# Batched 64x64 matrix products: the transpose of A moves from TensorE to 32x32 blocks on VectorE, with A loaded in tiles of 64 matrices

## The chip, the cores and the metric

The kernel runs on one core of one Trainium2 chip. The metric is the device time of one execution in microseconds (us); lower is better. Engines in the profile: PE is TensorE (PEld its weight loads), DVE is VectorE, ACT is ScalarE, POOL is GpSimd, SP is the engine that only issues transfers. SP, ACT and POOL each issue DMAs into a queue of their own: q1 is SP's, q10 is ACT's, q0 is POOL's. [...]

## The reference

```python
def setup_inputs():
    return {
        "a": np.random.randn(1024, 64, 64).astype(np.float32),
        "b": np.random.randn(1024, 64, 64).astype(np.float32),
    }

def reference(a, b):
    return np.matmul(a, b).astype(np.float32)
```

There are 1024 products of 64x64 matrices. Each of a, b and the output is 16.78 MB.

## The kernel before, in words

The batch is worked in 16 tiles of 64 matrices (index t). One TensorE multiply handles four matrices at once: the contraction index k is kept as 32 pairs of bf16 numbers (a pair is moved about as one fp32 word), four matrices times 32 pairs fill the 128 partitions, and the stationary operand is a block diagonal `at_bd` that holds the transposed a of those four matrices, with zeros elsewhere. The moving operand is b in bf16, `b_bf`. For each group of four there are two row halves (j) and two members of the pair (u), so 64 multiplies (L189) for each tile.

*a* comes in super-tiles of 128 matrices (index s, two tiles each). A super-tile has four parts h of 512 KB. `load_a` (L69) loads three parts with a cast to bf16 on POOL's queue (L73) and one part raw, in fp32, on SP's queue (L77). The first super-tile comes raw in all four parts, two on SP and two on ACT (L90). Every run that is read is 4 KB. `regroup` (L99) puts the parts together in one bf16 tile `a_bf`: for s = 0 by two copies each on VectorE and ScalarE (L105), else by two VectorE copies (L108, L111). `transpose` then uses TensorE with an identity (L120), eight 128x128 fp32 transposes for each half j, into PSUM, and ScalarE copies them out to `at_sb` (L123). `spread` (L133) copies `at_sb` into the block diagonal, four VectorE copies of 32 partitions for each tile. Two block diagonals are used in turn.

*b* comes one tile at a time, 1 MB, even tiles on SP and odd tiles on ACT (L96), with three buffers. `cast` turns it into bf16 on VectorE (L144), for the first tile on ScalarE, for the last tile in quarters on both (L149, L151).

*The output.* `multiply` writes two PSUM tiles for each t. Each is evacuated by four copies of 64x512 into `o_sb` (L177), on ScalarE but for two in each odd tile, which are VectorE's. `store` sends 1 MB for each tile from POOL's queue (L166), the last two tiles from SP and ACT in pieces. There are eight `o_sb` buffers.

The order of the instructions on every engine is the order of the program text: the schedule is written out by hand under `manual_schedule`, and each engine works its own list in order, waiting where its data isn't there. In the loop over t the next tile's spread and cast come first, then the loads further ahead, then `multiply(t)`, then regrouping and transposes for later super-tiles, then the store of tile t-1.

Of the kernel before, what the change touches and what calls it, by code (L numbers as in the profile page):

```python
# [7 lines left out]

fp32 = mybir.dt.float32
# [4 lines left out]
def kernel(  # L14
# [8 lines left out]

    nc = tc.nc
    B, M, K = a.shape  # L30
    _, _, N = b.shape
    assert (M, K, N) == (64, 64, 64) and B % 128 == 0

    n_t, n_s = B // 64, B // 128
    A_AHEAD = 3
    B_AHEAD = 3
    N_BD = 2
    HOLD = 2

    a_v = a.rearrange("(s g h) (mp v) k -> s h g mp (v k)", h=4, g=32, v=16)  # L40
    b_v = b.rearrange("(t g h) (kp u) n -> t (h kp) g (u n)", h=4, g=16, u=2)
    o_v = out.rearrange("(t gh x) (mo w) n -> t (x mo) gh (w n)", gh=8, x=8, w=4)

    consts = ctx.enter_context(tc.tile_pool(name="consts", bufs=1))
    a_pool = ctx.enter_context(tc.tile_pool(name="a_pool", bufs=A_AHEAD))
    b_pool = ctx.enter_context(tc.tile_pool(name="b_pool", bufs=B_AHEAD))
    work = ctx.enter_context(tc.tile_pool(name="work", bufs=2))
    o_pool = ctx.enter_context(tc.tile_pool(name="o_pool", bufs=8))
    t_psum = ctx.enter_context(
        tc.tile_pool(name="t_psum", bufs=4, space=bass.MemoryType.PSUM)  # L50
    )
    o_psum = ctx.enter_context(
        tc.tile_pool(name="o_psum", bufs=2, space=bass.MemoryType.PSUM)
    )

    bd_tiles = [
        consts.tile([128, 2, 16, 2, 4, 16], fp32, name=f"at_bd{i}") for i in range(N_BD)
    ]
    identity = consts.tile([128, 128], fp32)
    warm = consts.tile([128, 2], fp32)  # L60
    a_tiles, b_tiles, abf_tiles, at_tiles, bbf_tiles = {}, {}, {}, {}, {}
    held = {}

    def store_queue(t, lo):
        if t < n_t - 2:
            return nc.gpsimd
        return nc.scalar if t == n_t - 1 and lo % 4 == 0 else nc.sync

    def load_a(s):  # L69

        a_sb = a_pool.tile([128, 3, 16, 64], bf16, name="a_sb")
        for h in range(3):
            nc.gpsimd.dma_start(  # L73
                out=a_sb[:, h, :, :].rearrange("p v k -> p (v k)"), in_=a_v[s, h], single_packet=True
            )
        a_raw = a_pool.tile([128, 16, 64], fp32, name="a_raw")
        nc.sync.dma_start(out=a_raw[:].rearrange("p v k -> p (v k)"), in_=a_v[s, 3])  # L77
        a_tiles[s] = a_sb, a_raw

    def load_first_a():  # L80

        raw = [
            o_pool.tile([128, 8, 2, 2, 64], fp32, name="o_sb")[:].rearrange(
                "p gh j wl n -> p (gh j wl n)"
            )
            for _ in range(2)
        ]
        parts = [raw[h % 2][:, 1024 * (h // 2) : 1024 * (h // 2) + 1024] for h in range(4)]
        for h in range(4):
            (nc.scalar if h % 2 else nc.sync).dma_start(out=parts[h], in_=a_v[0, h])  # L90
        a_tiles[0] = parts

    def load_b(t):
        b_sb = b_pool.tile([128, 16, 128], fp32, name="b_sb")
# [1 line left out]
        queue.dma_start(out=b_sb[:], in_=b_v[t])  # L96
        b_tiles[t] = b_sb

    def regroup(s):  # L99
        a_sb = a_tiles.pop(s)  # L100
        a_bf = work.tile([128, 16, 4, 64], bf16, name="a_bf")
        if s == 0:
            for h in range(4):
                copy = nc.scalar.copy if h % 2 else nc.vector.tensor_copy
                copy(a_bf[:, :, h, :], a_sb[h].rearrange("p (v k) -> p v k", v=16))  # L105
        else:
            cast_sb, raw = a_sb
            nc.vector.tensor_copy(  # L108
                a_bf[:, :, 0:3, :], cast_sb[:].rearrange("p h v k -> p v h k")
            )  # L110
            nc.vector.tensor_copy(a_bf[:, :, 3, :], raw[:])  # L111
        abf_tiles[s] = a_bf
        at_tiles[s] = work.tile([128, 2, 32, 2, 4, 4], fp32, name="at_sb")

    def transpose(s, j):
        a_cols = abf_tiles[s][:].rearrange("p v h k -> p v (h k)").bitcast(fp32)
        for wl in range(2):
            at_ps = t_psum.tile([128, 4, 128], fp32, name="at_ps")
            for vo in range(4):
                nc.tensor.transpose(  # L120
                    at_ps[:, vo, :], a_cols[:, 4 * vo + 2 * j + wl, :], identity[:]
                )
            nc.scalar.copy(  # L123
                at_tiles[s][:, j, :, wl, :, :],
                at_ps[:].rearrange("p vo (g mp) -> p g mp vo", mp=4),
            )

    def spread(t):
        half = slice(16 * (t % 2), 16 * (t % 2) + 16)
        bd = bd_tiles[t % N_BD]  # L130
        for h in range(4):
            rows = slice(32 * h, 32 * h + 32)
            nc.vector.tensor_copy(  # L133
                bd[rows, :, :, :, h, :].rearrange("p j g wl mo -> p j (g wl) mo"),
                at_tiles[t // 2][rows, :, half, :, :, :].rearrange(
                    "p j g wl mp vo -> p j (g wl) (mp vo)"
                ),
            )

    def cast(t):  # L140
# [15 lines left out]
            piece()  # L156

    def multiply(t):
        at_bd = bd_tiles[t % N_BD][:].rearrange("p j g wl h mo -> p j g (wl h mo)")
        at_bd = at_bd.bitcast(bf16).rearrange("p j g (c u) -> p j g c u", u=2)  # L160
        b_bf = bbf_tiles.pop(t)
        last = t == n_t - 1
# [6 lines left out]
            )  # L169

        def evacuate(o_ps, gh, n, copies):

            for par in range(2):
                for wl in range(2):
                    src = o_ps[64 * wl : 64 * wl + 64, :, par, :, :]
                    dst = o_sb[64 * par : 64 * par + 64, gh : gh + n, :, wl, :]
                    copies[2 * par + wl](dst, src)  # L177

        for half in range(2):
            if not last:  # L180
                o_ps = o_psum.tile([128, 4, 2, 2, 64], fp32, name="o_ps")
            for g8 in range(8):
                if last and g8 % 4 == 0:
                    o_ps = t_psum.tile([128, 2, 2, 2, 64], fp32, name="at_ps")
                g = 8 * half + g8
                gl = (g8 % 4 if last else g8) // 2
                for j in range(2):
                    for u in range(2):
                        nc.tensor.matmul(  # L189
                            o_ps[:, gl, g % 2, j, :],  # L190
                            at_bd[:, j, g, :, u],
                            b_bf[:, g, 64 * u : 64 * u + 64],
                            start=(u == 0),
                            stop=(u == 1),
                        )
                if last and g8 % 4 == 3:
                    copy = nc.scalar.copy if g8 == 3 else nc.vector.tensor_copy
                    evacuate(o_ps, g // 4 * 2, 2, [copy] * 4)
            if not last:
                copies = [nc.scalar.copy] * 4  # L200
                if half and t % 2:
                    copies[2:] = [nc.vector.tensor_copy] * 2
                evacuate(o_ps, 4 * half, 4, copies)
        if last:
            held[t] = [lambda q=q: put(2 * q, 2) for q in range(4)]
        else:
# [1 line left out]
            held[t] = [lambda q=q: put(q, 8 if whole else 4) for q in ([0] if whole else [0, 4])]  # L208

    with tc.manual_schedule():  # L210
        load_first_a()

        nc.vector.memset(warm[:, 0:1], 0.0)
        nc.scalar.copy(warm[:, 1:2], warm[:, 0:1])  # L214
        load_b(0)
        load_b(1)
        nc.vector.memset(bd_tiles[0][:], 0.0)  # L217
        make_identity(nc, identity)
        nc.gpsimd.memset(bd_tiles[1][:, 0], 0.0)
        load_a(1)  # L220
        load_b(2)
        nc.gpsimd.memset(bd_tiles[1][:, 1], 0.0)
        load_a(2)
        regroup(0)
        transpose(0, 0)
        transpose(0, 1)
        spread(0)
        cast(0)
        for t in range(n_t):
            s, half = t // 2, t % 2  # L230
            if t + 1 < n_t:
                spread(t + 1)
                cast(t + 1)
            if t + B_AHEAD < n_t:
                load_b(t + B_AHEAD)
            if half == 0 and 0 < s < n_s - 1 - A_AHEAD:
                load_a(s + 1 + A_AHEAD)
            if half == 0 and 0 < s < n_s - 1:
                transpose(s + 1, 1)
            multiply(t)  # L240
            if t == 0:
                regroup(1)
                load_a(A_AHEAD)
                load_a(A_AHEAD + 1)
                transpose(1, 0)
                transpose(1, 1)
            elif t == 1:
                regroup(2)
            elif half == 0 and s + 2 < n_s:
                regroup(s + 2)  # L250
            if half == 1 and s + 2 < n_s:
                transpose(s + 2, 0)
            if t >= HOLD - 1:
                store(t - HOLD + 1)
        for t in range(n_t - HOLD + 1, n_t):
            store(t)
# [30 lines left out]
```

## Time and profile before

| | |
|---|---|
| time, median of 3 runs | 134.95 us (134.95 to 135.0) |
| span of the profiled execution, first to last instruction | 133.4 us |
| time of the profiled execution itself | not given apart from its span |
| busy: PE, DVE, ACT, POOL | 64.4, 94.6, 87.9, 33.0 us |
| moved in HBM | 33.55 MB read, 16.78 MB written |
| mean granted TensorE clock | 0.785 of full |

A group row of the page reads: line, engine, operation, output <- input, shapes, count, then busy us and mean ns of one, then the idle time of the engine just before these instructions and what ended most of it. In the strip of 40 slices each digit is a busy share in tenths.

### The profile page before, as it was taken

To read this page: it belongs to the slowest core of one execution; us is meant where nothing else is said; L and a number is where in the kernel's file an instruction comes from. 1 tells how busy PE (TensorE), PEld (TensorE's weight loads), DVE (VectorE), ACT (ScalarE), POOL (GpSimd) and SP (SyncE) were. 2 spreads that over 40 slices of the span, in tenths; PEclk is the share of its full clock that TensorE was granted. 3 is DMA by queue.
4 is the path that set the end of the run, shared out by engine and by line. 5 is a ranking of instruction groups with operands and counts; after the bars stand their busy time and mean duration, and the time that the engine had idled before them with its cause. 6 is when DMAs were issued, how large, how long until landed. Compare 5 with 4: busy or idle time off the path is not lost.

```text
span 133.4 us, 2837 instructions
## 1 busy us (share of the span) xinstructions
PE 64.4 (48%) x1152; PEld 61.1 (46%) x1152; DVE 94.6 (71%) x120; ACT 87.9 (66%) x161; POOL 33.0 (25%) x43
## 2 busy tenths in 40 slices
PE   0006406960089384289518970956197363970000
PEld 0006306950089274189418950945196363960000
DVE  5930399109998809995999699959999995987000
ACT  3225424999036998969595969696968969099600
POOL 8991000420090070341233021203020410300000
PEclk9999975797557999856985699599959955599555
DMA  3999999999999999999999999999999999999990
GB/s 77 371 329 311 307 311 281 284 306 325 327 312 401 316 320 333 399 384 397 311 281 375 406 389 351 304 316 390 394 396 387 396 392 391 402 405 398 382 319 18
DMA packets 19021, 45.01 MB, mean 337 GB/s; under 512 B 1088, under 2 KB 3136, under 8 KB 19008
## 3 DMA queue, kind: packets, MB, share of 16 engines
q0 software_dynamic: 6832, 20.19, 50.1%
q1 hardware_dynamic: 7120, 14.68, 30.4%
q10 hardware_dynamic: 5056, 9.96, 19.7%
q8 instruction: 9, 0.15, 0.4%
q14 instruction: 4, 0.03, 0.1%
HBM read 33.55 MB, written 16.78 MB: 377 GB/s over the span
## 4 chain that ended last, share of the span: by engine, by line
DMA 53%; DVE 15%; ACT 13%; PE 6%; issue 5%; SPq 2%; DVEq 0%; ACTq 0%
DMA b_sb<-in_b_dram 53%; ACT o_sb L177 9%; DVE at_bd L133 6%; PE o_ps L189 4%; DVE b_bf L144 4%; DVE o_sb L177 3%; PE at_ps L120 2%; ACT at_sb L123 2%; ACT b_bf L144 1%; SPq L90 1%; DVE a_bf L108 1%; SPq L96 1%; ACT b_bf L151 1%; DVE a_bf L111 0%; SPq L77 0%
## 5 line engine op out<-in xcount | busy, mean ns | idle before, releaser
L177 ACT COPY o_sb<-o_ps 64x512 f32<-64x512 f32 x106 | 61.5, 580 | 10.3 <-PE o_ps L189 9.0
L189 PEld LDWEIGHTS <-at_bd 128*128 128x128 bf16 x1024 | 42.3, 113 | 39.5 <-DVE b_bf L144 25.7
L189 PE MATMUL o_ps<-b_bf,at_bd 128*128 128x64 bf16 x960 | 42.6, 216 | 35.4 <-DVE b_bf L144 23.4
L133 DVE COPY at_bd<-at_sb 32x1024 f32<-32x1024 f32 x64 | 46.9, 733 | 14.1 <-ACT at_sb L123 11.8
L120 PE MATMUL at_ps<-identity,a_bf 128*128 128x128 f32 x128 | 21.2, 335 | 19.4 <-ACT a_bf L105 11.2
L166 POOL DMA_DIRECT2D out_dram<-o_sb x14 | 15.4, 1097 | 56.9 <-ACT at_sb L123 23.4
L120 PEld LDWEIGHTS at_ps<-identity,a_bf 128*128 128x128 f32 x128 | 19.3, 180 | 19.5 <-issue 19.5
L123 ACT COPY at_sb<-at_ps 128x512 f32<-128x512 f32 x32 | 17.5, 590 | 11.0 <-PE at_ps L120 7.8
L144 DVE CAST b_bf<-b_sb 128x2048 bf16<-128x2048 f32 x14 | 17.8, 1271 | 9.6 <-DMA b_sb<-in_b_dram 9.4
L73 POOL DMA_DIRECT2D a_sb<-in_a_dram x21 | 13.6, 662 | 26.4 <-DVE a_bf L108 19.4
L177 DVE COPY o_sb<-o_ps 64x512 f32<-64x512 f32 x14 | 9.7, 690 | 0.3
L108 DVE COPY a_bf<-a_sb 128x3072 bf16<-128x3072 bf16 x7 | 6.7, 950 | 0.0
L105 ACT CAST a_bf<-o_sb 128x1024 bf16<-128x1024 f32 x2 | 2.1, 1044 | 5.2 <-DMA o_sb<-in_a_dram 5.2
L111 DVE CAST a_bf<-a_raw 128x1024 bf16<-128x1024 f32 x7 | 4.8, 683 | 0.0
L144 ACT CAST b_bf<-b_sb 128x2048 bf16<-128x2048 f32 x1 | 1.9, 1900 | 3.9 <-DMA b_sb<-in_b_dram 3.9
L105 DVE CAST a_bf<-o_sb 128x1024 bf16<-128x1024 f32 x2 | 2.8, 1382 | 1.9 <-DMA o_sb<-in_a_dram 1.9
L217 DVE MEMSET at_bd<- 128x4096 f32 x1 | 3.5, 3472 | 0.8 <-issue 0.8
L177 DVE COPY o_sb<-at_ps 64x256 f32<-64x256 f32 x8 | 3.4, 422 | 0.5 <-PE at_ps L189 0.4
L151 ACT CAST b_bf<-b_sb 128x512 bf16<-128x512 f32 x2 | 1.1, 615 | 3.6 <-DMA b_sb<-in_b_dram 3.6
L177 ACT COPY o_sb<-at_ps 64x256 f32<-64x256 f32 x8 | 2.9, 366 | 0.1
L214 ACT ACT_TABLE_LOAD x1 | 1.3, 1283 | 2.3 <-issue 2.3
L189 PE MATMUL at_ps<-b_bf,at_bd 128*128 128x64 bf16 x64 | 2.0, 193 | 1.0 <-DVE at_bd L133 1.0
(12 smaller groups left out, 6.1 us busy)
## 6 DMA issues: line engine op xcount, KB each, us to landing
out_dram<-o_sb POOLq DMA_DIRECT2D x14, 1024.0 KB, 21.6
a_sb<-in_a_dram POOLq DMA_DIRECT2D x21, 256.0 KB, 16.4
a_raw<-in_a_dram SPq DMA_DIRECT2D x7, 512.0 KB, 18.7
o_sb<-in_a_dram SPq DMA_DIRECT2D x2, 512.0 KB, 5.9
o_sb<-in_a_dram ACTq DMA_DIRECT2D x2, 512.0 KB, 7.1
out_dram<-o_sb SPq DMA_DIRECT2D x2, 512.0 KB, 7.5
out_dram<-o_sb SPq DMA_DIRECT2D x2, 256.0 KB, 7.8
out_dram<-o_sb ACTq DMA_DIRECT2D x2, 256.0 KB, 5.5
```

The costliest lines, as they stand in the source:

```text
L73: nc.gpsimd.dma_start(out=a_sb[:, h, :, :].rearrange("p v k -> p (v k)"), in_=a_v[s, h], single_packet=True)
L105: copy(a_bf[:, :, h, :], a_sb[h].rearrange("p (v k) -> p v k", v=16))
L108: nc.vector.tensor_copy(a_bf[:, :, 0:3, :], cast_sb[:].rearrange("p h v k -> p v h k"))
L111: nc.vector.tensor_copy(a_bf[:, :, 3, :], raw[:])
L120: nc.tensor.transpose(at_ps[:, vo, :], a_cols[:, 4 * vo + 2 * j + wl, :], identity[:])
L123: nc.scalar.copy(at_tiles[s][:, j, :, wl, :, :], at_ps[:].rearrange("p vo (g mp) -> p g mp vo", mp=4),)
L133: nc.vector.tensor_copy(bd[rows, :, :, :, h, :].rearrange("p j g wl mo -> p j (g wl) mo"), at_tiles[t // 2][rows, :, half, :, :, :].rearrange(
L144: (nc.vector.tensor_copy if t else nc.scalar.copy)(b_bf[:], b_sb[:])
L166: store_queue(t, lo).dma_start(out=o_v[t, :, lo : lo + n, :], in_=o_sb[:, lo : lo + n].rearrange("p gh j wl n -> p (gh j wl n)"),)
L177: copies[2 * par + wl](dst, src)
L189: nc.tensor.matmul(o_ps[:, gl, g % 2, j, :], at_bd[:, j, g, :, u], b_bf[:, g, 64 * u : 64 * u + 64], start=(u == 0), stop=(u == 1),)
L217: nc.vector.memset(bd_tiles[0][:], 0.0)
```

## The change

The super-tile of 128 matrices is given up: a comes tile by tile, 64 matrices in two parts h of 512 KB. The partition order of a part is now (q mp g) and no longer (g mp): the 32 partitions of one quadrant hold four row blocks mp of eight matrices, so that a 32x32 block transpose within a quadrant brings the pairs of k onto the partitions. VectorE does this transpose, one instruction for each part over 128 partitions and 512 fp32 words, and writes it so that the four `spread` copies read one contiguous stretch. TensorE's transposes, the identity, the PSUM tiles for them, ScalarE's copies out of PSUM and `regroup` are gone.

Ten of the 32 parts come raw (both of tile 0, the second of each odd tile) in a pool of three buffers, and are cast by ScalarE (one by VectorE); the other 22 are cast on POOL's queue. Loads of a run six tiles ahead; before, three super-tiles. All evacuations but those of the last tile are on ScalarE. PSUM has three output tiles in place of two, and two smaller ones for the last tile. In the start, POOL's casting loads come ahead of its memsets.

```diff
-    A_AHEAD = 3
+    A_AHEAD = 6
+    RAW = [(0, 0), (0, 1)] + [(t, 1) for t in range(1, n_t, 2)]
-    a_v = a.rearrange("(s g h) (mp v) k -> s h g mp (v k)", h=4, g=32, v=16)
+    a_v = a.rearrange("(t h g q) (mp v) k -> t h (q mp) g (v k)", h=2, g=8, q=4, mp=4)
...
+    def load_a(t):
+        a_tiles[t] = a_pool.tile([128, 2, 16, 64], bf16, name="a_sb")
+        for h in range(2):
+            if (t, h) in RAW:
+                raw = raw_pool.tile([128, 16, 64], fp32, name="a_raw")
+                raw_tiles[t, h] = raw
+                queue = nc.scalar if t == 0 and h else nc.sync
+                queue.dma_start(out=raw[:].rearrange("p v k -> p (v k)"), in_=a_v[t, h])
+            else:
+                nc.gpsimd.dma_start(
+                    out=a_tiles[t][:, h].rearrange("p v k -> p (v k)"),
+                    in_=a_v[t, h],
+                    single_packet=True,
+                )
...
+    def transpose(t):
+        a_sb = a_tiles.pop(t)
+        at_tiles[t] = work.tile([128, 2, 8, 4, 4, 4], fp32, name="at_sb")
+        for h in range(2):
+            if (t, h) in RAW:
+                copy = nc.vector.tensor_copy if t == 0 and not h else nc.scalar.copy
+                copy(a_sb[:, h], raw_tiles.pop((t, h))[:])
+            pairs = a_sb[:, h].rearrange("p v k -> p (v k)").bitcast(fp32)
+            nc.vector.transpose(
+                at_tiles[t][:, h].rearrange("p g w mp vo -> p w vo mp g"),
+                pairs.rearrange("p (vo w kp) -> p w vo kp", vo=4, w=4),
+            )
+
+    def spread(t):
+        bd = bd_tiles[t % N_BD]
+        at_sb = at_tiles.pop(t)
+        for q in range(4):
+            rows = slice(32 * q, 32 * q + 32)
             nc.vector.tensor_copy(
+                bd[rows, :, :, q, :, :].rearrange("p g w mp vo -> p (g w) (mp vo)"),
+                at_sb[rows].rearrange("p h g w mp vo -> p (h g w) (mp vo)"),
             )
...
-                copies = [nc.scalar.copy] * 4
-                if half and t % 2:
-                    copies[2:] = [nc.vector.tensor_copy] * 2
-                evacuate(o_ps, 4 * half, 4, copies)
+                evacuate(o_ps, 4 * half, 4, [nc.scalar.copy] * 4)
...
     with tc.manual_schedule():
+        load_a(0)
         nc.vector.memset(warm[:, 0:1], 0.0)
         nc.scalar.copy(warm[:, 1:2], warm[:, 0:1])
         load_b(0)
+        load_a(1)
         load_b(1)
         nc.vector.memset(bd_tiles[0][:], 0.0)
         load_b(2)
         load_a(2)
+        nc.gpsimd.memset(bd_tiles[1][:, 0:8], 0.0)
+        load_a(3)
+        nc.gpsimd.memset(bd_tiles[1][:, 8:16], 0.0)
+        load_a(4)
+        load_a(5)
+        transpose(0)
         spread(0)
         cast(0)
+        transpose(1)
         for t in range(n_t):
             if t + 1 < n_t:
                 spread(t + 1)
                 cast(t + 1)
+            if t + 2 < n_t:
+                transpose(t + 2)
             if t + B_AHEAD < n_t:
                 load_b(t + B_AHEAD)
+            if t + A_AHEAD < n_t:
+                load_a(t + A_AHEAD)
             multiply(t)
             if t >= HOLD - 1:
                 store(t - HOLD + 1)
```

More of the change, by code (lines that the diff above doesn't have):

```diff
@@ L5 @@
 from concourse import bass_utils, mybir
-from concourse.masks import make_identity
 from concourse._compat import with_exitstack
@@ L31 @@
     _, _, N = b.shape
-    assert (M, K, N) == (64, 64, 64) and B % 128 == 0
-    n_t, n_s = B // 64, B // 128
-    A_AHEAD = 3
+    assert (M, K, N) == (64, 64, 64) and B % 64 == 0
+    n_t = B // 64
+    A_AHEAD = 6
     B_AHEAD = 3
@@ L38 @@
     HOLD = 2
-    a_v = a.rearrange("(s g h) (mp v) k -> s h g mp (v k)", h=4, g=32, v=16)
-    b_v = b.rearrange("(t g h) (kp u) n -> t (h kp) g (u n)", h=4, g=16, u=2)
+    RAW = [(0, 0), (0, 1)] + [(t, 1) for t in range(1, n_t, 2)]
+    a_v = a.rearrange("(t h g q) (mp v) k -> t h (q mp) g (v k)", h=2, g=8, q=4, mp=4)
+    b_v = b.rearrange("(t g q) (kp u) n -> t (q kp) g (u n)", q=4, g=16, u=2)
     o_v = out.rearrange("(t gh x) (mo w) n -> t (x mo) gh (w n)", gh=8, x=8, w=4)
@@ L45 @@
     a_pool = ctx.enter_context(tc.tile_pool(name="a_pool", bufs=A_AHEAD))
+    raw_pool = ctx.enter_context(tc.tile_pool(name="raw_pool", bufs=3))
     b_pool = ctx.enter_context(tc.tile_pool(name="b_pool", bufs=B_AHEAD))
@@ L48 @@
     o_pool = ctx.enter_context(tc.tile_pool(name="o_pool", bufs=8))
-    t_psum = ctx.enter_context(
-        tc.tile_pool(name="t_psum", bufs=4, space=bass.MemoryType.PSUM)
-    )
-    o_psum = ctx.enter_context(
-        tc.tile_pool(name="o_psum", bufs=2, space=bass.MemoryType.PSUM)
+    o_psum = ctx.enter_context(
+        tc.tile_pool(name="o_psum", bufs=3, space=bass.MemoryType.PSUM)
+    )
+    q_psum = ctx.enter_context(
+        tc.tile_pool(name="q_psum", bufs=2, space=bass.MemoryType.PSUM)
     )
     bd_tiles = [
-        consts.tile([128, 2, 16, 2, 4, 16], fp32, name=f"at_bd{i}") for i in range(N_BD)
+        consts.tile([128, 16, 4, 4, 4, 4], fp32, name=f"at_bd{i}") for i in range(N_BD)
     ]
-    identity = consts.tile([128, 128], fp32)
     warm = consts.tile([128, 2], fp32)
-    a_tiles, b_tiles, abf_tiles, at_tiles, bbf_tiles = {}, {}, {}, {}, {}
-    held = {}
+    a_tiles, raw_tiles, at_tiles = {}, {}, {}
+    b_tiles, bbf_tiles, held = {}, {}, {}
     def store_queue(t, lo):
@@ L67, in store_queue @@
         return nc.scalar if t == n_t - 1 and lo % 4 == 0 else nc.sync
[L69 to L91, printed above, removed]
+    def load_a(t):
[12 more added lines that the diff above has]
+                )
     def load_b(t):
@@ L97, in load_b @@
         b_tiles[t] = b_sb
[L99 to L125, printed above, removed]
+    def transpose(t):
[9 more added lines that the diff above has]
+                pairs.rearrange("p (vo w kp) -> p w vo kp", vo=4, w=4),
@@ L126, in transpose @@
             )
     def spread(t):
-        half = slice(16 * (t % 2), 16 * (t % 2) + 16)
         bd = bd_tiles[t % N_BD]
-        for h in range(4):
-            rows = slice(32 * h, 32 * h + 32)
+        at_sb = at_tiles.pop(t)
+        for q in range(4):
+            rows = slice(32 * q, 32 * q + 32)
             nc.vector.tensor_copy(
[L134 to L137, printed above, removed]
+                bd[rows, :, :, q, :, :].rearrange("p g w mp vo -> p (g w) (mp vo)"),
+                at_sb[rows].rearrange("p h g w mp vo -> p (h g w) (mp vo)"),
@@ L158, in multiply @@
     def multiply(t):
-        at_bd = bd_tiles[t % N_BD][:].rearrange("p j g wl h mo -> p j g (wl h mo)")
+        at_bd = bd_tiles[t % N_BD][:].rearrange("p g (j wl) q mp vo -> p j g (wl q mp vo)", j=2)
         at_bd = at_bd.bitcast(bf16).rearrange("p j g (c u) -> p j g c u", u=2)
@@ L183, in multiply @@
                 if last and g8 % 4 == 0:
-                    o_ps = t_psum.tile([128, 2, 2, 2, 64], fp32, name="at_ps")
+                    o_ps = q_psum.tile([128, 2, 2, 2, 64], fp32, name="q_ps")
                 g = 8 * half + g8
@@ L210 @@
     with tc.manual_schedule():
-        load_first_a()
+        load_a(0)
         nc.vector.memset(warm[:, 0:1], 0.0)
@@ L215 @@
         load_b(0)
+        load_a(1)
         load_b(1)
         nc.vector.memset(bd_tiles[0][:], 0.0)
-        make_identity(nc, identity)
-        nc.gpsimd.memset(bd_tiles[1][:, 0], 0.0)
-        load_a(1)
         load_b(2)
-        nc.gpsimd.memset(bd_tiles[1][:, 1], 0.0)
         load_a(2)
-        regroup(0)
-        transpose(0, 0)
-        transpose(0, 1)
+        nc.gpsimd.memset(bd_tiles[1][:, 0:8], 0.0)
[4 more added lines that the diff above has]
+        transpose(0)
         spread(0)
         cast(0)
+        transpose(1)
         for t in range(n_t):
-            s, half = t // 2, t % 2
             if t + 1 < n_t:
@@ L233 @@
                 cast(t + 1)
+            if t + 2 < n_t:
+                transpose(t + 2)
             if t + B_AHEAD < n_t:
                 load_b(t + B_AHEAD)
[L236 to L239, printed above, removed]
+            if t + A_AHEAD < n_t:
+                load_a(t + A_AHEAD)
             multiply(t)
[L241 to L252, printed above, removed]
             if t >= HOLD - 1:
```

## The prediction

> **What bounds the kernel now.** I read the page's strip of 40 slices first, then the queue table, then the windows of the DMA engines, then the chain of waits.
>
> ```profile
> DMA  3999999999999999999999999999999999999990
> HBM read 33.55 MB, written 16.78 MB: 377 GB/s over the span
> ```
>
> The DMA engines are busy from the first slices to the last but one: 50.33 MB (33.55 + 16.78) in a span of 133.4 us. The windows (columns: stretch, length, busy us of PE, PEld, DVE, ACT and POOL, PE clock, DMA share, GB/s) show whether that is a steady rate:
>
> ```profile
> 2.00:5.00 3.00, 0.00 (x0) 0.00 (x0) 3.00 (x1) 1.47 (x3) 3.00 (x5) 1.00 0.90 259
> 10.00:20.00 10.00, 3.60 (x16) 3.38 (x17) 4.36 (x7) 4.10 (x6) 0.53 (x1) 0.90 1.08 310
> 90.00:100.00 10.00, 6.04 (x132) 5.83 (x133) 9.71 (x13) 7.78 (x15) 2.30 (x2) 0.83 1.03 393
> 100.00:110.00 10.00, 5.94 (x120) 5.49 (x119) 9.68 (x13) 8.26 (x17) 1.90 (x2) 0.84 1.03 391
> 117.00:124.00 7.00, 2.22 (x68) 1.97 (x65) 5.21 (x12) 6.82 (x14) 0.00 (x0) 0.99 1.02 400
> 129.00:133.40 4.40, 0.00 (x0) 0.00 (x0) 0.00 (x0) 0.00 (x0) 0.00 (x0) 0.50 0.19 68
> ```
>
> The GB/s count what is written. A casting load reads twice what it writes: the software queue wrote 0.93 MB of casts in 10 to 20 us, so 3.10 + 0.93 = 4.03 MB were read or stored, 403 GB/s. So every full stretch shown stands at 391 to 403, whatever the mix. With 398, 50.33 MB take 126.5 us. The other 6.9 us lie at the ends: before 5 us 0.78 MB moved (worth 2.0 us, so 3.0 lost), after 129 us 0.30 MB (4.4 less 0.75, so 3.65 lost). Start, transfers, end: 3.0 + 126.5 + 3.65 = 133.2 of 133.4.
>
> How the queues share, in 15 to 20 us (columns: packets, MB, share of 16 engines' time):
>
> ```profile
> q0 software_dynamic: 257, 0.46, 48.7%
> q1 hardware_dynamic: 257, 0.65, 36.2%
> q10 hardware_dynamic: 235, 0.45, 23.6%
> ```
>
> Busy queues get equal packets. In 117 to 124 us q0 alone has 97% and the rate stays at 400, so one queue that is never empty is enough.
>
> The end is a chain behind the last load: b of tile 15 is awaited by L151 until 116.88, and the span ends 16.5 us later. All DMA ends about 130 too, so both run out together. Hence the rule that I use: span = the later of (start + 126.5 + end) and (last load used + 16.5).
>
> **Engines, part by part.** The rows that price the change:
>
> ```profile
> L177 ACT COPY o_sb<-o_ps 64x512 f32<-64x512 f32 x106 | 61.5, 580 | 10.3 <-PE o_ps L189 9.0
> L133 DVE COPY at_bd<-at_sb 32x1024 f32<-32x1024 f32 x64 | 46.9, 733 | 14.1 <-ACT at_sb L123 11.8
> L120 PE MATMUL at_ps<-identity,a_bf 128*128 128x128 f32 x128 | 21.2, 335 | 19.4 <-ACT a_bf L105 11.2
> L123 ACT COPY at_sb<-at_ps 128x512 f32<-128x512 f32 x32 | 17.5, 590 | 11.0 <-PE at_ps L120 7.8
> L144 DVE CAST b_bf<-b_sb 128x2048 bf16<-128x2048 f32 x14 | 17.8, 1271 | 9.6 <-DMA b_sb<-in_b_dram 9.4
> L177 DVE COPY o_sb<-o_ps 64x512 f32<-64x512 f32 x14 | 9.7, 690 | 0.3
> L111 DVE CAST a_bf<-a_raw 128x1024 bf16<-128x1024 f32 x7 | 4.8, 683 | 0.0
> ```
>
> *TensorE* loses 128 transposes, 64.4 - 21.2 = 43.2 us. It bounds nothing; worth nothing.
>
> *ScalarE* loses L123 (17.5) and two casts at L105 (2.1), and gains 14 evacuations (8.1) and nine raw casts at L105's 1.04 (9.4): 87.9 becomes 85.8. Per tile 8 x 0.580 + half of 1.04 = 5.2 us. The raw cast now stands ahead of a tile's evacuations, so a late raw load would hold these; it is issued four tiles early, and such loads landed in 18.7 us at the median.
>
> *VectorE* loses L108 (6.7), L111 (4.8), L105 (2.8) and 14 evacuations (9.7). It gains one raw cast (0.7) and 32 block transposes of 128x512 fp32, which no row shows. Below, they are bounded by half of the 128x1024 cast at L111, 0.34 us; above, by the slowest copy of up to 1024 elements, one L105 cast of 2.07 us. The row of as many elements read once is the evacuation of 64x512 at 0.69 us, and I take it: 32 x 0.69 = 22.1. DVE: 94.6 - 24.0 + 22.8 = 93.4 us. Per tile: 4 x 0.733 + 1.27 + 2 x 0.69 = 5.6 us; with 0.34, 4.9; with 2.07, 8.3.
>
> [...]
>
> *The spread* keeps its 64 copies at 0.73 us, in runs of 16 elements on both sides as before.
>
> **Transfers.** Bytes read and written in HBM are the same; one 512 KB part of a turns from raw to cast (22 casts, 10 raw). From the shares in 15 to 20 us a cast packet (4 KB read) costs 0.487 x 16 x 5 / 257 = 152 ns; a 4 KB store packet in 90 to 100 us (61.1% for 611 packets) costs 0.611 x 160 / 611 = 160 ns. Nothing to gain or lose. Runs stay 4 KB; their order in HBM changes. No row prices that. For all 16.78 MB of a (42.2 us) I bound it by the spread of the rates shown, 391 to 403, 3% or 1.3 us either way, and take zero, since no mix shown left that band.
>
> *Start.* POOL's first cast is issued at 3.00 us, behind the identity and a memset, and q0 moved nothing before 5 us. Now it is POOL's first work, about 0.7 us, so its packets can fill the 0.19 MB missing in 3 to 5 us: 0.5 us gained (bounds 0 and the whole hole of 2 to 5 us, 1.05).
>
> *Do the engines still feed the queues?* SP moved 2.1 MB until b of tile 0 landed at 19.26, about 121 GB/s; now half of that a goes ahead of it, 1.57 MB, 13 us, so tile 0 multiplies near 17 instead of 21.24. Loads ahead are six tiles of a and three of b, 9.4 MB or 24 us: enough. Then engines need 5.6 us a tile and DMA 50.33 / 16 / 0.398 = 7.9, so DMA sets the pace. In one software queue the casts for tile u+2 stand behind stores up to u-6. So at tile 13, a whole (16.8), b of 15 tiles (15.7) and 8 stores (8.4) must have moved: 40.9 MB, 3.0 + 102.8 = 105.8 us (before, this multiply began at 107.8). One DVE tile later, 111.4, b of tile 15 is cast, against 116.88 now; plus 16.5 is 127.9, under the DMA's end. So the end is pure DMA, with the last stores issued earlier into a full queue. Of the 3.65 us at the end, the ragged part is at most the 2 us before the wait after the last packet; I take 0.4.
>
> DMA_DIRECT2D for casts and stores stay on POOL (21 + 14 become 22 + 14, 0.66 us each for the casts), raw loads on SP (now eight more than the first tile's, before seven); a raw load waiting for its three buffers holds SP's next b, but those buffers are freed two tiles after landing. [...] Measured: in 90 to 100 us DVE was busy 9.71 of 10 and q0 moved 2.33 MB at a DMA share of 1.03. [...]
>
> **Sum.** 133.4 - 0.5 (start) - 0.4 (end) = 132.5. The runs' median, 134.95, lies 1.55 above the span (the page gives no time of its own for the profiled execution, so I take that one at the median): 134.05, said as 134.1.
>
> **Rivals.**
> 1. *Nothing moves.* The holes at both ends are latencies, not late issues: 134.95. For it: q10 and q1 were both loaded from 0.75 us, yet nothing moved before 2 us. What a measurement can tell is 0.2%, 0.27 us. Chance 0.13.
> 2. *Slower by slow transposes.* The strided writes double the row's 0.69 or worse. DVE waits become the pace when tile 15's cast comes after 117: (117 - 19) / 14 = 7.0 us a tile, that is (7.0 - 4.2) / 2 = 1.4 us a transpose. Each 0.1 us beyond costs 28 x 0.1 = 2.8 us: 1.5 gives 138, 2.07 gives 154. Against: one read and one write per element in every row near. Chance 0.13.
> 3. *Slower by late casts.* DVE's transpose waits in line ahead of the next spread and cast of b, PE and ACT behind it. Before, the casts were up to eight tiles ahead; now six, and their slowest landing was 29 us. If they take that, plus 8 us behind a store's wait, five tiles last 37 us, 7.4 each: tile 15 at 17 + 14 x 7.4 = 120.6, span 137.1, time 138.6; half-way, 136.5. Against: while q0 is late it gets more of the engines, as in 117 to 124. Chance 0.17.
> 4. *The order of a in HBM counts.* 1.3 us: 135.4 when worse (0.07), 132.8 when better, within the forecast's cases.
>
> **Numbers.** My forecast (faster, 132 to 134.7) gets 0.50. Faster 0.50, same 0.13, slower 0.13 + 0.17 + 0.07 = 0.37. Range: low is 134.95 less 1.05 and 2.0, 131.9, said as 132.0; the high end takes in rival 3 and the transposes up to 1.5 us: 138.6. The forecast's own range is 132.0 to 134.7.
>
> **What would show it.** DMA share above 1.0 from 5 to 129 us; q0 with packets before 4 us; tile 0's multiply near 17; transposes at 0.6 to 0.8 us; DVE near 93; the last cast of b before 117. Wrong if the transposes exceed 1.4 us, if DMA falls under 1.0 in mid-span, or if full stretches leave 391 to 403 GB/s.

## The result, and the profile after

The changed kernel takes 140.91 us (median of 4 runs, 140.02 to 142.28) against 134.97. The run at 142.28 was in a slower state of the chip, so the differences below use the median of the other three, 140.55. The change makes the kernel slower by 5.6 us, a ratio of 1.041 (95% interval 1.036 to 1.045). Forecast were 134.1 us and a range up to 138.6. The profiled execution has a span of 138.6 us and a time of its own of 140.55; the span before was 133.4.

Two lines of the page, first the DMA strip, then what was moved:

```profile
DMA  3999999999999999999999999999999999999993
HBM read 33.55 MB, written 16.78 MB: 363 GB/s over the span
```

The strip looks as it did: busy from end to end. The bytes are the same too. They only moved at 363 GB/s of the span where it was 377. The windows of the changed kernel (columns as in the prediction) say where:

```profile
5.00:10.00 5.00, 0.00 (x0) 0.00 (x0) 4.18 (x4) 1.04 (x1) 3.79 (x5) 1.00 1.07 255
10.00:20.00 10.00, 0.00 (x0) 0.10 (x1) 3.82 (x6) 0.74 (x1) 1.24 (x2) 1.00 1.09 292
100.00:110.00 10.00, 4.29 (x78) 3.97 (x75) 8.96 (x12) 7.71 (x15) 0.89 (x1) 0.50 1.06 337
117.00:124.00 7.00, 3.93 (x91) 3.69 (x88) 6.38 (x12) 5.17 (x9) 0.89 (x1) 0.74 1.03 407
129.00:138.60 9.60, 0.00 (x0) 0.00 (x0) 0.00 (x0) 0.00 (x0) 0.00 (x0) 0.50 0.81 276
```

The DMA share is above 1.0 in every full stretch, as forecast. But the rate has left the band. In 10 to 20 us POOL's queue wrote 0.91 MB, all of it casts, so 2.92 + 0.91 = 3.83 MB were read, 383 GB/s against 403 before. In 5 to 10 us it is 1.27 + 0.45 = 1.72 MB, 344 GB/s, against 1.81 + 0.25 = 2.06 MB and 412. Once all of a has been loaded, in 117 to 124 us, the rate is 407, as good as the 400 before. The engines of DMA are as busy as they were and get less done while a is being loaded. They do so in some stretches more than in others. In 40 to 50 us the packet records of the trace have 0.54 MB of casts before the change and 0.42 MB after it, so with these lines, first before and then after, the rates are 400 and 342:

```profile
40.00:50.00 10.00, 7.20 (x149) 6.76 (x147) 5.55 (x7) 8.61 (x15) 2.89 (x5) 0.90 1.06 346
```

```profile
40.00:50.00 10.00, 4.97 (x88) 4.55 (x86) 8.06 (x11) 9.75 (x18) 3.41 (x5) 1.00 1.06 300
```

The queue view shows it packet by packet. ACT's queue carries nothing but b in 30 to 40 us, in packets of 2 KB, and b's loads are the same in both kernels. First the kernel before, then the changed one (columns: packets, MB, share of 16 engines' time):

```profile
DMA packets 1305, 3.21 MB, mean 321 GB/s; under 512 B 128, under 2 KB 128, under 8 KB 1305
...
q10 hardware_dynamic: 300, 0.58, 15.2%
```

```profile
DMA packets 1200, 3.29 MB, mean 329 GB/s; under 512 B 79, under 2 KB 79, under 8 KB 1199
...
q10 hardware_dynamic: 342, 0.67, 24.1%
```

The share times 160 us (16 engines for 10 us), divided by the packets, is the mean time of one. A packet of b takes 0.152 x 160 / 300 = 0.081 us before and 0.241 x 160 / 342 = 0.113 us after. GB/s alone can't be compared here, since the mix of casts and stores differs; the time of one packet of the same load can. Over the whole run the packet records of the trace give the same: raw packets of 4 KB on SP's queue 198 ns (176 before), tile 0's raw part on ACT's queue 281 (167 for the two there before), b on ACT's queue 98 (86), casts 172 and 172. (The shares give a little less, as in the prediction's 152 ns for a cast: they also count the packets of 4 bytes, 16 for each load or store, at 9 to 16 ns each.)

The engines did what the groups were to show, with one exception:

```profile
L146 ACT COPY o_sb<-o_ps 64x512 f32<-64x512 f32 x120 | 69.6, 580 | 10.6 <-PE o_ps L158 9.0
L105 DVE COPY at_bd<-at_sb 32x1024 f32<-32x1024 f32 x64 | 44.5, 695 | 2.3
L95 DVE STREAM_TRANSPOSE at_sb<-a_sb 128x512 f32<-128x512 f32 x32 | 32.6, 1079 | 10.9 <-ACT a_sb L93 10.8
```

The evacuations cost 580 ns each as before. The block transposes cost 1.08 us, not 0.69, so VectorE is busy for 102.9 us and not 93.4.

### The profile page after: what moved, and what is told of

It is laid out like the page before. It is cut to its first block, busy times and chain, and to the rows that moved or that the text cites. A ratio compares the mean times of both kernels' runs of the same rounds, so it can differ in the third digit from the quotient of the medians.

```text
span 138.6 us, 2542 instructions
## 1 busy us (share of the span) xinstructions
PE 54.3 (39%) x1024; PEld 51.7 (37%) x1024; DVE 102.9 (74%) x123; ACT 86.6 (62%) x150; POOL 31.1 (22%) x42
## 4 chain that ended last, share of the span: by engine, by line
DMA 74%; DVE 9%; ACT 8%; issue 1%; PE 1%; DVEq 0%; SPq 0%; ACTq 0%
DMA b_sb<-in_b_dram 50%; DMA a_raw<-in_a_dram 24%; ACT o_sb L146 6%; DVE b_bf L114 4%; DVE at_sb L95 2%; DVE at_bd L105 2%; ACT a_sb L93 2%; DVE o_sb L146 1%; PE q_ps L158 1%; ACT b_bf L121 0%; DVEq L235 0%; ACT b_sb L84 0%; SPq L84 0%; DVEq L105 0%; ACTq L121 0%
## 5 line engine op out<-in xcount | busy, mean ns | idle before, releaser
L158 PEld LDWEIGHTS <-at_bd 128*128 128x128 bf16 x1024 | 51.7, 126 | 75.4 <-DVE b_bf L114 42.9
L158 PE MATMUL o_ps<-b_bf,at_bd 128*128 128x64 bf16 x960 | 51.2, 235 | 68.6 <-DVE b_bf L114 44.3
L146 ACT COPY o_sb<-o_ps 64x512 f32<-64x512 f32 x120 | 69.6, 580 | 10.6 <-PE o_ps L158 9.0
L105 DVE COPY at_bd<-at_sb 32x1024 f32<-32x1024 f32 x64 | 44.5, 695 | 2.3
L95 DVE STREAM_TRANSPOSE at_sb<-a_sb 128x512 f32<-128x512 f32 x32 | 32.6, 1079 | 10.9 <-ACT a_sb L93 10.8
L93 ACT CAST a_sb<-a_raw 128x1024 bf16<-128x1024 f32 x9 | 9.4, 1046 | 13.7 <-DMA a_raw<-in_a_dram 13.5
L146 DVE COPY o_sb<-q_ps 64x256 f32<-64x256 f32 x8 | 3.4, 422 | 3.5 <-PE q_ps L158 3.4
L158 PE MATMUL q_ps<-b_bf,at_bd 128*128 128x64 bf16 x64 | 3.1, 216 | 4.3 <-DVE o_sb L146 1.9
L146 ACT COPY o_sb<-q_ps 64x256 f32<-64x256 f32 x8 | 2.9, 367 | 0.1
L121 ACT CAST b_bf<-b_sb 128x512 bf16<-128x512 f32 x2 | 1.1, 617 | 2.0 <-DMA b_sb<-in_b_dram 2.0
L188 POOL MEMSET at_bd<- 128x2048 f32 x1 | 1.9, 1863 | 0.0
L186 POOL MEMSET at_bd<- 128x2048 f32 x1 | 1.8, 1848 | 0.0
```

What stands on the lines that cost most here:

```text
L93: copy(a_sb[:, h], raw_tiles.pop((t, h))[:])
L95: nc.vector.transpose(at_tiles[t][:, h].rearrange("p g w mp vo -> p w vo mp g"), pairs.rearrange("p (vo w kp) -> p w vo kp", vo=4, w=4),)
L105: nc.vector.tensor_copy(bd[rows, :, :, q, :, :].rearrange("p g w mp vo -> p (g w) (mp vo)"), at_sb[rows].rearrange("p h g w mp vo -> p (h ...
L158: nc.tensor.matmul(o_ps[:, gl, g % 2, j, :], at_bd[:, j, g, :, u], b_bf[:, g, 64 * u : 64 * u + 64], start=(u == 0), stop=(u == 1),)
L186: nc.gpsimd.memset(bd_tiles[1][:, 0:8], 0.0)
L188: nc.gpsimd.memset(bd_tiles[1][:, 8:16], 0.0)
```

## The experiments

Two theories stood at first. *Transfer theory*: the order in which a is read slows the DMA engines; nothing else matters. *Engine theory*: the longer transposes and ScalarE's waits for raw parts pace the loads. In the diffs below `a_v` is the view of a that the loads read; the first dimension that steps over partitions is called outer, the second inner. Except with runs of 2 KB, a kernel that reads a in another order multiplies permuted rows and doesn't give the reference's output: it measures the loads and is no replacement.

**All parts contiguous.** Only the order of a's 4 KB pieces is altered.

```diff
-    a_v = a.rearrange("(t h g q) (mp v) k -> t h (q mp) g (v k)", h=2, g=8, q=4, mp=4)
+    a_v = a.rearrange("(t h g q) (mp v) k -> t h (g q mp) (v k)", h=2, g=8, q=4, mp=4)
```

> The changed kernel, with only the order in which the parts of a are read altered: each 512 KB part is now one contiguous stretch of HBM, partition p taking the p-th 4 KB (the products then belong to other rows of a). Instructions, bytes and waits are the same. Transfer theory (the order of a's loads slows the DMA engines; a raw 4 KB packet took 198 ns on SP's queue against 176 before, and b's packets 97 against 86 on ACT's): time 134 to 136, raw packets near 175 ns. Engine theory (VectorE's transposes at 1.08 us and ScalarE's waits for raw parts pace the loads): stays at 140 to 141.

Measured: 133.68 us, ratio to the kernel before 0.990 (0.987 to 0.992). The same instructions with the same 1.08 us transposes are now faster than the kernel before. The engine theory falls, and the whole loss, 140.55 - 133.68 = 6.9 us, lies in the order. The packet of b is back, in the same window of this kernel:

```profile
DMA packets 1404, 3.48 MB, mean 348 GB/s; under 512 B 91, under 2 KB 91, under 8 KB 1404
...
q10 hardware_dynamic: 262, 0.50, 13.3%
```

0.133 x 160 / 262 = 0.081 us. But "order" means two things: how far the pieces lie apart in HBM, and into how many groups the 128 partitions are cut. The next two tell them apart.

**16 groups of 8, the pieces of a group side by side.**

```diff
+    a_v = a.rearrange("(t x h r) (mp v) k -> t h x (r mp) (v k)", x=16, h=2, r=2, mp=4)
```

> The changed kernel with another order of a: outer dimension of 16 as in the change, inner dimension of 8, but the 8 pieces of 4 KB are neighbours in HBM (32 KB) and the outer step is 64 KB (rows of a are permuted). If the far steps inside a group (64 KB from piece to piece) are what costs, 134 to 136. If the cost is how 16 groups of 8 partitions are dealt to the 16 DMA engines, 140 to 141 as with the change. Engine theory: 140 to 141.

**32 groups of 4, the pieces of a group 256 KB apart.**

```diff
+    a_v = a.rearrange("(t j h i) (mp v) k -> t h (i mp) j (v k)", j=4, h=2, i=8, mp=4)
```

> The changed kernel with a third order of a: outer dimension of 32 as before the change, inner dimension of 4 whose pieces lie 256 KB apart (rows of a are permuted). If far steps in HBM cost, 140 or more. If the dealing of 16 groups of 8 partitions costs, 134 to 136. Engine theory: 140 to 141.

Measured: 16 groups of near pieces 140.88 us (ratio 1.042, 1.036 to 1.049), 32 groups of far pieces 134.22 (0.994, 0.992 to 0.996). With 16 groups it is the same whether the pieces are neighbours (140.88) or 64 KB apart (140.55; runs of both reach from 139.6 to 141.6). The distance in HBM is worth at most the half microsecond between 133.68 and 134.22, and most of that is there by 5 us: up to then 1.03 MB moved in the contiguous kernel and 0.86 MB with 32 groups, 0.4 us at 398 GB/s. Cutting the partitions into 16 groups of 8 is worth all the rest: 140.88 - 134.22 = 6.7 us.

**Two more cuts**, 8 groups of 16 and 64 groups of 2:

```diff
+    # 8 by 16
+    a_v = a.rearrange("(t j h i) (mp v) k -> t h (i mp) j (v k)", j=16, h=2, i=2, mp=4)
+    # 64 by 2
+    a_v = a.rearrange("(t j h i) (mp v) k -> t h (i mp) j (v k)", j=2, h=2, i=16, mp=4)
```

> The changed kernel with an order of a whose outer dimension is 8 and inner 16 (64 KB apart; rows of a are permuted). If the outer dimension is what is dealt to the DMA engines, only 8 of 16 work on a part: well over 145 us. [...]

> The changed kernel with an order of a whose outer dimension is 64 and inner 2, the two pieces 512 KB apart (rows of a are permuted). If every outer dimension from 32 up is dealt well, 133.5 to 134.5 like 32 by 4 (134.22) and 128 (133.68); if 32 by 4 was a special case, 138 or more; if far steps count for something, 135 to 137.

Measured: 172.3 us (a single run) with 8 groups, 134.38 (ratio 0.995, 0.994 to 0.997) with 64. So the row by outer dimension is 8: 172.3; 16: 140.9; 32: 134.2; 64: 134.4; one contiguous 128: 133.7. From 32 up nothing is lost, and the kernel before had 32.

**Which loads suffer.** Three kernels: few raw parts, raw parts contiguous with the casts left as they were, no raw part at all.

```diff
+    # few raw parts
+    RAW = [(0, 0), (0, 1)]
+    # no raw part
+    RAW = []
+    # raw parts contiguous: their DMA reads a_c[t, h] in place of a_v[t, h]
+    a_c = a.rearrange("(t h g q) (mp v) k -> t h (g q mp) (v k)", h=2, g=8, q=4, mp=4)
```

> The changed kernel with only the two parts of tile 0 raw; the other 30 parts are cast on POOL's queue, in the change's own order. Cast packets took 172 ns before and after, only raw packets and b's grew. If the raw loads in that order are what slows the engines, 135 to 137.5 (the two raw parts of tile 0 still cost some at the start). If the order costs casts as well, about 140. Engine theory: 1 us less at most, as ScalarE loses eight raw casts of 1.05 us: 139 to 141.

> The changed kernel with the ten raw parts read as contiguous stretches and the 22 casting loads left in the change's order (rows of a are permuted in the raw parts). If only raw loads suffer, 133.5 to 134.3 as with all parts contiguous (133.68). If casting loads suffer too, 135 to 136: with few raw parts 136.83 - 133.68 = 3.1 us were still missing, and it isn't known how much of that is the two raw parts of tile 0.

> The changed kernel with all 32 parts cast on POOL's queue in the change's order, the reference's output kept. If only raw loads suffer: the 2 raw parts of tile 0 cost as much each as the others, 136.83 - 1.0 = 135.8, or less if the slow start of 5 to 10 us goes with them, 134 to 136. If the casting loads suffer as well, 136.5 to 138. The first tile waits for casts on one queue, which the transfers hide.

Measured: few raw 136.83 (ratio 1.013, 1.011 to 1.016); raw contiguous 134.74 (0.999, 0.998 to 1.000); no raw 136.02 (1.008, 1.006 to 1.011). With all 22 casts left in 16 groups only 134.74 - 133.68 = 1.1 us are lost, 0.05 a part. The ten raw parts lose 140.55 - 134.74 = 5.8 us, 0.6 a part; such a part would take 0.524 MB / 398 GB/s = 1.3 us at the full rate. That is an average: by the packet records SP's nine raw parts took from 167 to 254 ns a packet in the changed kernel, and no run shows why some were spared. Raw loads from SP and ACT suffer, casting loads hardly. The "only raw loads" theory was nearly right for the contiguous case, which fell between the two forecasts, and expected 134 to 136 without raw parts; 136.02 is at its edge. In that kernel all 32 parts are cast in 16 groups from the start, and the start is slow: in 10 to 20 us its POOL queue wrote 0.93 MB of casts, as in the kernel before, but all queues together 2.83 MB, not 3.10.

**The kernel before, spoiled.** Only its seven raw parts on SP's queue are read in the change's order.

```diff
+    a_w = a.rearrange("(s c g q) (mp v) k -> s c (q mp) g (v k)", c=4, g=8, q=4, mp=4)
-        nc.sync.dma_start(out=a_raw[:].rearrange("p v k -> p (v k)"), in_=a_v[s, 3])
+        nc.sync.dma_start(out=a_raw[:].rearrange("p v k -> p (v k)"), in_=a_w[s, 3])
```

> The kernel before, with the seven raw parts on SP's queue read in the order of the change (outer 16, inner 8, 64 KB apart; the products then belong to other rows of a); TensorE's transposes stay. Dealing theory (a raw load whose outer dimension is 16 slows the DMA engines, in whatever kernel): taking eight raw parts away gave 136.83 from 140.91, 0.5 us a part, so 135.0 + 3.6, 137.5 to 139.5, raw packets near 200 ns. If the slow loads need something else of the change (VectorE's transposes, ScalarE's raw casts), 135.0 stays.

Measured: 139.11 us, ratio 1.031 (1.029 to 1.033): 4.15 us for seven parts, 0.6 each, as in the changed kernel. TensorE's transposes are still there, VectorE's are not. Its view of 30 to 40 us:

```profile
DMA packets 1082, 2.72 MB, mean 272 GB/s; under 512 B 98, under 2 KB 98, under 8 KB 1082
...
q10 hardware_dynamic: 315, 0.61, 25.7%
```

0.257 x 160 / 315 = 0.131 us for a packet of b, on a queue that nobody touched, instead of 0.081. A load in 16 groups slows its neighbours as well.

**Runs of 2 KB.** This kernel's layout needs a quadrant of 32 partitions for each of four neighbouring matrices, so 32 groups of 4 are to be had, with the views of b and of the output left as they are, only with shorter runs.

```diff
+    a_r = a.rearrange("(t h c g q) (mp v) k -> t h c (q mp) g (v k)", h=2, c=2, g=4, q=4, mp=8)
...
-                queue.dma_start(out=raw[:].rearrange("p v k -> p (v k)"), in_=a_v[t, h])
+                for c in range(2):
+                    queue.dma_start(out=raw[:, c].rearrange("p v k -> p (v k)"), in_=a_r[t, h, c])
```

> The changed kernel with the reference's output kept: each raw part comes by two loads of 256 KB in runs of 2 KB, outer dimension of 32 (four matrices by eight blocks of eight rows), inner of 4; VectorE transposes a raw part by two instructions of 256 words and writes them to the same places. Dealing theory: outer 32 is as good as before, 133.5 to 135.5, at the price of ten more transposes of about half size (10 x 0.1 us of fixed cost, VectorE not the bound). If small runs or the change's casts cost, 135.5 to 137. Theory of far steps in HBM (refuted above): 140.

Measured: 137.6 us (ratio 1.020, 1.018 to 1.021), a miss: better than the change by about 3 us, short of the 133.5 to 135.5 expected. Part of what is missing to the 134.22 of 32 groups is lost early: in 10 to 20 us 2.83 MB were written, 0.93 MB of them casts, which makes 376 GB/s against 403 with 32 groups. The kernel without raw parts has 376 there too, and its casts also run in 16 groups. More is lost at the end:

```profile
118.00:124.00 6.00, 3.35 (x64) 3.23 (x64) 4.52 (x6) 2.86 (x6) 0.89 (x1) 0.54 1.03 404
124.00:130.00 6.00, 2.60 (x61) 2.52 (x62) 3.85 (x9) 5.13 (x12) 0.00 (x0) 0.75 0.86 308
```

From 124 us the DMA share falls to 0.86: the last tile is multiplied from 125.48 to 130.4, and the stores run dry ahead of it. That small runs are the cause is not shown. One reason that fits is that busy queues got equal packets in the kernel before (257 on q0 and 257 on q1 in 15 to 20 us), so that a raw load in packets of 2 KB would get half the bytes for its turn and the tiles come later; no run isolates that. The 0.1 us taken for each further transpose does not show: in this kernel's trace two transposes of 128x256 together take 1.11 us and one of 128x512 takes 1.12.

**The strides of the transposes.** On the contiguous kernel, the transposes write one word after the other.

```diff
-                at_tiles[t][:, h].rearrange("p g w mp vo -> p w vo mp g"),
+                at_tiles[t][:, h].rearrange("p g w mp vo -> p (g w mp vo)").rearrange("p (w vo c) -> p w vo c", w=4, vo=4),
```

> The changed kernel with contiguous parts of a (133.68 us in the run before) and, in addition, transposes that write their 512 words one after the other in place of steps of 256 and 16 bytes (the values then stand in other places of the block diagonal). If the steps make the transposes 1.08 us, they fall to 0.6 to 0.7; if 1.08 is the operation's own rate, they stay. In time: if transfers are the bound, 133.4 to 134.0 either way, though VectorE loses 12 us of work; if VectorE had become a second bound, 131.5 to 133.

```profile
L95 DVE STREAM_TRANSPOSE at_sb<-a_sb 128x512 f32<-128x512 f32 x32 | 21.0, 690 | 9.6 <-ACT a_sb L93 9.5
```

Measured: 690 ns a transpose in place of 1077, VectorE 92.5 us in place of 103.4, and 133.89 us against 133.68. The steps cost 0.39 us a transpose, 12 us for the 32 (VectorE's busy time falls by 10.9), and the time doesn't notice: transfers are the bound.

**The start by itself**, in the kernel before:

```diff
+        load_a(1)
         make_identity(nc, identity)
         nc.gpsimd.memset(bd_tiles[1][:, 0], 0.0)
-        load_a(1)
```

> The kernel before with one edit: POOL issues the casting loads of the second super-tile ahead of the identity and of its first memset. This is the start term of the prediction by itself, 0.5 us (bounds 0 and 1.05): 134.0 to 134.9. If the loads of SP and ACT alone set the start, 134.9 to 135.1; if the later identity delays the first transposes into a wait of the queues, 135.2 or more.

Measured: 134.61 us, ratio 0.998 (0.997 to 1.000): 0.35 us, which lies within the bounds of the term. But its profile doesn't show the term. POOL issues its first cast at 1.3 us and not at 3.0, and the first packet comes at 5.51 us and not at 7.05, some 4 us after the issue both times; before 5 us there is none, and 2 to 5 us move no more than the 259 GB/s of the kernel before:

```profile
2.00:5.00 3.00, 0.00 (x0) 0.00 (x0) 3.00 (x1) 1.47 (x3) 2.92 (x5) 1.00 0.86 255
```

Where the 0.35 us come from stays open. It is the only version with the reference's output that came out ahead of both kernels, and only by as much as can just be told from nothing.

## Why the prediction was wrong, point by point

*The bound* was right. Transfers set the time before and after; in the contiguous kernel 12 us less of VectorE's transposes didn't move it.

*The step that failed* is the one on transfers, "Runs stay 4 KB; their order in HBM changes. No row prices that", with its 1.3 us either way and zero taken; rival 4 was that same term, with 0.07. It asked about addresses in HBM and was right about those. It didn't see that the view of a also changes how a load is cut: (g mp) has an outer dimension of 32, (q mp) one of 16. That shape costs 6.7 us, five times the bound. The band of 391 to 403 GB/s could not bound it, since every load of the kernel before had a good shape: a rate that no row contradicts is no bound for a shape that no row contains. (The band was narrow for its own kernel too: 5 to 10 us stood at 412 there.) The sign of the forecast failed with this term.

The prediction's own test named the failure: "if full stretches leave 391 to 403 GB/s". The other test beside it, a DMA share under 1.0, would have missed it. The share is made of the packets' own durations, so it stays above 1.0 when each packet takes longer: in 10 to 20 us of the changed kernel the three queues' packets make 48.0 + 34.5 + 26.2%, a share of 1.09, at 383 GB/s. The signs that were to come with the gain failed in the changed kernel: POOL's queue had its first packet at 6.41 us, tile 0 was multiplied at 21.2 and the last b was cast at 118.7.

*The end and the chain of tiles hold* once the shape is mended. The kernel with 32 groups, as before the change, took 134.22 us, and the forecast was 134.1; that it comes so near is partly luck, as the next point shows. In the contiguous kernel the chain is the one that was worked out. From its list of L121 (first and last start in us) and from its windows:

```profile
L121 ACT CAST b_bf<-b_sb x2: 614/616/619, 111.8 to 112.3; 128x512 bf16<-128x512 f32 x2
```

```profile
2.00:5.00 3.00, 0.00 (x0) 0.00 (x0) 3.00 (x1) 0.67 (x2) 3.00 (x4) 1.00 0.85 321
129.00:131.70 2.70, 0.00 (x0) 0.00 (x0) 0.00 (x0) 0.00 (x0) 0.00 (x0) 0.50 0.34 118
```

The last b was cast at 111.8 (worked out: 111.4), the first tile multiplied from 18.2 (near 17), and the last store was issued at 121.0 and not 125.85. Its span, 131.7, is even 0.8 below the 132.5 of the sum.

*The start* did not go as told. POOL's packets were to fill the hole before 5 us, for 0.5 us. They came at 5.42 us with 32 groups and at 5.00 in the contiguous kernel, where POOL's queue moved two packets before 5 us. The 321 GB/s of the contiguous kernel in 2 to 5 us, against 259, are SP's and ACT's: SP's first packets came at 1.76 us, against 2.15 with 32 groups, and ACT's at 2.80, against 4.05. By 5 us the contiguous kernel had moved 1.03 MB, not 0.78, worth 0.6 us. That is near the 0.5 taken, but for another reason: luck, and the kernel with 32 groups got only 0.2 us of it (0.86 MB). The kernel before with only POOL's loads moved ahead, 255 GB/s, shows none of it.

*The transposes* were mis-sized: 0.69 taken, 1.08 measured, within the bounds of 0.34 and 2.07 and below the 1.4 at which rival 2 decides. Written without steps they take 0.69, the row that was chosen; the steps are the difference, 0.39 us a transpose.

*Rival 3*, late casts, can be ruled out as the cause: the DMA share never fell below 1.03 between 10 and 124 us, and the same schedule with contiguous parts ends 7 us earlier. ScalarE's waits for raw parts (13.5 us in the changed kernel) remain at 10.7 in the contiguous one and cost nothing there.

*Why 16 groups are slow* is not settled. The guess put on record for 8 groups, that only 8 of the 16 engines would work on a part, had "well over 145 us", and 172.3 came; in the trace each of that kernel's ten raw loads leaves 8 packets of 4 bytes, where each with 16 and with 32 groups leaves 16. That these packets count the engines is the author's reading and not shown, and by them 16 and 32 groups are alike, where the runs show 140.9 and 134.2. Why a load in 16 groups costs more, and why a casting load loses 0.05 us where a raw one loses 0.6, no run here shows: the trace doesn't name the engine of a packet.

## What to carry to other kernels

When a change touches the view that a DMA reads, compare its outer dimension before and after, not only its run length and bytes: here 32 and 64 over 128 partitions took 134.2 and 134.4 us and a contiguous load 133.7, but 16 took 140.9 and 8 took 172.3. To find such a loss, don't look at the busy share (1.07 before and 1.05 after in 30 to 40 us); take a load that the change left alone and compare the time of one of its packets (81 and 113 ns there). And this transfer-bound kernel could afford a slower instruction (12 us of strided transposes: 133.68 us with the steps, 133.89 without) but not one slower class of loads: ten loads of 0.5 MB were enough for 4%.

## What the runs showed of the hardware that had not been expected

The same 512 KB, in the same 4 KB runs, cost 0.6 us more for each raw load in 16 groups of 8 partitions than in 32 groups of 4, and only 0.05 us more for a casting load (against a contiguous one). A load in the bad shape also lengthens the packets of a load beside it on another queue, from 81 to 113 and 131 ns. How far the pieces lay apart in HBM, 4 KB or 256 KB, mattered by half a microsecond in 134 at most.
